# Expert weights loaded as one consecutive 8 KB run per partition, with the features permuted to match

## The chip, the cores and the metric

One program on one core of a Trainium2 chip. The metric is the device time of one execution in microseconds (us), from the first to the last instruction with what lies around them. The core has TensorE (PE; its weight loads are listed apart as PEld), VectorE (DVE), ScalarE (ACT), GpSimd (POOL) and SyncE (SP, which here issues nearly all DMAs), a 128-partition on-chip memory (SBUF), an accumulator memory that PE writes (PSUM), and 16 DMA engines.

## The reference, cut to what matters

One encoder layer over 256 tokens of 1024 features: a norm, three mixing branches, a residual; then a norm, a router and a mixture of 16 experts (4 groups of 4, every token goes to 2 experts of one group), a residual and a last norm. All is float32. The change touches the experts alone:

```python
t = h.reshape(b * s, d)                                   # 256 tokens x 1024
...
for g in range(g_n):                                      # 4 groups
    a = jnp.einsum('td,edf->tef', t, w_gate[g])           # 4 experts x (1024 x 512)
    u = jnp.einsum('td,edf->tef', t, w_up[g])             # 4 experts x (1024 x 512)
    hid = jax.nn.silu(a) * u * combine[:, g, :, None]
    out = out + jnp.einsum('tef,efd->td', hid, w_down[g]) # 4 experts x (512 x 1024)
```

The weights of the 16 experts are 100.7 MB (16 x 3 x 1024 x 512 x 4 bytes) and are read once.

## The kernel before, in words

The program first runs the mixing branches (up to about 300 us). Then it works out the output projection and the router (to about 320 us), and then the experts in 8 pairs `p` (to about 532 us).

**Order of work.** The expert stage is written in program order: every engine runs its instructions in the order of the code. `experts` calls, for each pair, `gate_up` for the even expert, `hidden` of the pair before (PE transposes that turn the activations `gs` so that features lie on partitions, result `hh`), `down` of the pair before, and `gate_up` for the odd expert, with `scatter` and `place` (adding the results back to the tokens' sums) in its middle. After every second pair `gather` makes the four experts' inputs: PE multiplies the normed tokens by a 0/1 matrix `X` and so collects at most 64 tokens for each expert into `xg`, with features on partitions. The normed tokens are kept in two parts, `x1_hi` (written by ACT in `normed_hi`) and `x1_lo` (the rest, written by DVE in `normed_lo`), in tiles C2 and E1; the raw ones are `x1` (tile C1). At the first `gather` all `x1_hi` products run first, then `normed_lo` runs on DVE, then the `x1_lo` products.

**Weights.** A stock of 20 SBUF buffers of 1 MB (8 KB on each partition; tags r0.., B0.., E0.., G.., h0.. and so on) holds weights. `plan` is the list of loads in order of use, one per buffer; `fetch(tag)` issues the next load of the plan into a buffer that has been used up, on SP's queue, and `take` hands out the oldest loaded buffer. A gate/up buffer holds 256 rows of gate and the same 256 rows of up as two DMAs of 512 KB: row r of a 128-row block goes to partition r, so that each run of consecutive bytes in one partition is one row, 2 KB. A down buffer holds 256 rows of 4 KB. `gate_up` takes four buffers in turn and gives each back after its four products (two 128-row blocks, each for gate and up). Gate goes to PSUM partitions 0 to 63 and up to 64 to 127. A float32 product is two PE instructions in the trace, so a buffer is 8 of them. ACT then writes silu of the gate into the tile `gs`, DVE multiplies it by the up part (the last two lines of `gate_up`).

**Before the experts.** SP loads the router's weights (`wr`, 20 columns) around 198 us, DVE scales them by the gain of the norm. The gains lie in `gt` (partition p, column k: feature 128k + p), loaded at the start; `gather` applies the same gain when it moves `xg` out of PSUM.

**The end.** The last pair ends with `down_1` and `scatter_1` over column halves, then `finish` norms the rows and stores them.

Of the kernel before, what the change touches and what calls it, by code (L numbers as in the profile page):

```python
# [9 lines left out]
F32 = mybir.dt.float32  # L10
# [4 lines left out]
AF = mybir.ActivationFunctionType  # L15
ALU = mybir.AluOpType
# [14 lines left out]
def hybrid_encoder_kernel(  # L31
# [112 lines left out]
        plan.pop(0)(raw)  # L144
        ready.append((tag, raw))

    def rows_in(src, parts=1):
        def go(raw):
            dst = raw.rearrange("p (k n) -> p k n", n=src.shape[1])
            k = dst.shape[1] // parts  # L150
            for i in range(parts):
                feeder[0].dma_start(
                    dst[:, i * k : i * k + k], src[i * k * P : (i + 1) * k * P].rearrange("(k p) n -> p k n", p=P)
                )

        return go

# [566 lines left out]
    raw_tags.append("B1")  # L724
    wr = wp.tile([P, KT, 32], F32, tag="gs", name="wr")
    V.memset(wr, 0.0)
    tc.keep_in_program_order(nc.sync.dma_start(wr[:, :, 16:20], w_rg[0].rearrange("(k p) n -> p k n", p=P)))
    tc.keep_in_program_order(nc.sync.dma_start(wr[:, :, 0:16], w_re[0].rearrange("(k p) n -> p k n", p=P)))
    for k in range(KT):
# [34 lines left out]
    def expert_units():  # L764
        us = []

        def gate_and_up(e, r):
            def go(raw):
                for h, w in ((0, w_gate), (1024, w_up)):
                    rows_in(w[e, r : r + 256])(raw[:, h : h + 1024])  # L770

            return go

        def gu(e):
            us.extend(gate_and_up(e, r) for r in range(0, D, 256))

        def dn(*es):
            for r in (0, 256):
                us.extend(rows_in(w_down[e, r : r + 256]) for e in es)

        def dn_cols(e):
            for c in (0, 512):
                us.append(rows_in(w_down[e, :, c : c + 512], 2 if c and e == NE - 1 else 1))

        for p in range(NP):
            gu(2 * p)
            if p:
                dn(2 * p - 2, 2 * p - 1)
            gu(2 * p + 1)
        dn_cols(NE - 2)  # L790
        dn_cols(NE - 1)
        return us
# [181 lines left out]
    x1_hi = slot("C2", [P, 2, D], F32R)  # L974
    x1_lo = slot("E1", [P, 2, D], F32R)

    def normed_hi(a, n):
        ns = slice(n * 512, n * 512 + 512)
        A.activation(x1_hi[:, a, ns], x1[:, a, ns], AF.Copy, scale=r2[:, a : a + 1])

    def normed_lo(a, n):
        ns = slice(n * 512, n * 512 + 512)
        V.scalar_tensor_tensor(
            x1_lo[:, a, ns], x1[:, a, ns], r2[:, a : a + 1], x1_hi[:, a, ns].bitcast(F32), op0=ALU.mult, op1=ALU.subtract
        )

    for a in range(2):
# [128 lines left out]
    def gather(pd, lead=False):  # L1116
        pts = [bank([P, 2, 256]) for _ in range(4)]

        def part(u, x, first):
            for j in range(2):  # L1120
                ks = slice((2 * u + j) * P, (2 * u + j + 1) * P)
                for a in range(2):
                    PE.matmul(
                        pts[u][:, j],
                        x[:, a, ks],
                        pd[:, a].rearrange("p e s -> p (e s)"),
                        start=first and j + a == 0,
                        stop=not first and j + a == 2,
                    )
# [8 lines left out]
        for u in range(4):  # L1138
            pt = pts[u]
            if not lead:  # L1140
                part(u, x1_hi, True)
            part(u, x1_lo, False)
            if u % 2:
                for j in range(2):
                    k = 2 * u + j
                    A.activation(
                        xg[:, k].rearrange("p e s -> p (e s)"), pt[:, j], AF.Copy, scale=gt[:, 3, k : k + 1]
                    )
            else:
                V.tensor_tensor(  # L1150
                    xg[:, 2 * u : 2 * u + 2].rearrange("p k e s -> p k (e s)"),
                    pt,
                    gt[:, 3, 2 * u : 2 * u + 2].unsqueeze(2).to_broadcast([P, 2, 256]),
                    op=ALU.mult,
                )
        return xg
# [22 lines left out]
    def take(n):  # L1179
        tag, raw = ready.pop(0)  # L1180
        return tag, raw.rearrange("p (k n) -> p k n", n=n)

    def gate_up(xg, i, p, gs, between=None):
        pt = bank([P, DFF])
        for u in range(2):
            for h in range(2):
                tag, w = take(DFF)
                for j in range(2):
                    k = 4 * u + 2 * h + j
                    for c in range(2):  # L1190
                        PE.matmul(  # L1191
                            pt[c * 64 : c * 64 + 64], xg[:, k, p % 2 * 2 + i], w[:, 2 * c + j], start=k == 0, stop=k == KT - 1
                        )
                fetch(tag)
            if between and not u:
                between()
        gs = gs or keep([P, DFF], "gs")
        A.activation(gs[64:128], pt[0:64], AF.Silu)  # L1198
        V.tensor_mul(gs[i * 64 : i * 64 + 64], gs[64:128], pt[64:128])  # L1199
        return gs  # L1200

    def down(hs):
# [223 lines left out]
```

## Time and profile before

| | |
|---|---|
| time, median of 3 runs | 545.36 us (545.16 to 545.42) |
| the profiled execution | 545.44 us, span 543.5 us |
| granted PE clock, mean of the span | 0.994 of full speed |
| PE busy | 528.5 us, 97% of the span |
| DVE, ACT, POOL busy | 264.3, 229.0, 18.5 us |
| DMA | 159.91 MB, 89815 packets, mean 294 GB/s |

The span is the time from the first to the last instruction; 1.9 us lie around it. The profile also tells, for every idle stretch of an engine, what ended it, and for every stretch of time how busy the 16 DMA engines were and how many bytes they moved. PE is called busy while a product is in it, so its busy share says that it was fed and not that it ran at its peak.

### The profile page before, as it was taken

The numbers are of one execution on the slowest core, as the hardware profiler recorded it, in microseconds if no ns is written. First come the engines' busy times: TensorE is split into PE (matmuls) and PEld (weight loads), VectorE is DVE, ScalarE is ACT, GpSimd is POOL, SyncE is SP. The second block draws the span as 40 slices with busy tenths as digits, with TensorE's granted clock in tenths as the row PEclk, the third lists the DMA queues.
The fourth block names the chain that finished last, engine by engine and source line by source line (L and its number), as shares of the span: only waits on it lengthen the run. The fifth ranks groups of instructions, "written<-read, shape, count | busy, mean of one in ns | idle before, by whom it ended". The sixth has DMA issues, their size and how long they took to land. (4 is left out here: it accounts for less than half of the span.)

```text
span 543.5 us, 7482 instructions
## 1 busy us (share of the span) xinstructions
PE 528.5 (97%) x2912; PEld 359.9 (66%) x2912; DVE 264.3 (49%) x461; ACT 229.0 (42%) x378; POOL 18.5 (3%) x21
## 2 busy tenths in 40 slices
PE   8999999999999999999999999999999999999992
PEld 6999899967778888888888863353435343534340
DVE  6598798995657768384566171130112111210122
ACT  6775566698654464544535261121111111111123
POOL 0005000040000000000000000000000000000000
PEclk9999999999999999999999999999999999999997
DMA  8987778045445799739983799999999999999962
GB/s 302 390 316 233 224 147 256 17 156 163 148 154 189 235 334 301 257 103 403 354 318 151 275 344 330 416 406 418 406 414 409 409 413 407 416 406 418 406 242 81
DMA packets 89815, 159.91 MB, mean 294 GB/s; under 512 B 13104, under 2 KB 27824, under 8 KB 89776
## 3 DMA queue, kind: packets, MB, share of 16 engines
q1 hardware_dynamic: 89056, 158.80, 80.1%
q10 hardware_dynamic: 720, 0.58, 0.3%
q8 instruction: 25, 0.41, 0.3%
q14 instruction: 14, 0.11, 0.1%
HBM read 158.32 MB, written 1.05 MB: 293 GB/s over the span
## 5 line engine op out<-in xcount | busy, mean ns | idle before, releaser
L129 DVE TENSOR_TENSOR h<-r,h 128x1024 fp32r<-128x1024 f32 x58 | 71.2, 1239 | 31.6 <-ACT h L128 31.2
L128 ACT CAST h<-r 128x1024 fp32r<-128x1024 f32 x58 | 60.2, 1048 | 23.4 <-PE pj L308 12.5
L306 PE MATMUL pj<-h,A 128*128 128x512 f32 x160 | 63.1, 394 | 0.0
L308 PE MATMUL pj<-h,A 128*128 128x512 f32 x160 | 62.7, 392 | 0.0
L307 PE MATMUL pj<-h,A 128*128 128x512 f32 x160 | 62.6, 391 | 0.0
L1199 DVE TENSOR_TENSOR gs<-gs,b 64x512 f32<-64x512 f32 x16 | 11.1, 691 | 87.1 <-ACT gs L1198 87.1
L288 PE MATMUL pj<-A,h 128*128 128x256 f32 x160 | 45.7, 286 | 0.0
L290 PE MATMUL pj<-A,h 128*128 128x256 f32 x160 | 45.5, 284 | 0.0
L289 PE MATMUL pj<-A,h 128*128 128x256 f32 x160 | 45.3, 283 | 0.0
L308 PEld LDWEIGHTS pj<-h,A 128*128 128x128 f32 x160 | 30.1, 188 | 6.9 <-issue 0.8
L306 PEld LDWEIGHTS pj<-h,A 128*128 128x128 f32 x160 | 30.1, 188 | 6.7 <-issue 0.4
L307 PEld LDWEIGHTS pj<-h,A 128*128 128x128 f32 x160 | 30.1, 188 | 6.3 <-DVE h L129 0.4
L1230 DVE SCALAR_TENSOR_TENSOR os<-b,c,os 128x512 fp32r<-128x512 f32 x16 | 12.0, 751 | 41.9 <-ACT os L1229 41.0
L1198 ACT ACTIVATE gs<-b 64x512 f32<-64x512 f32 x16 | 9.4, 588 | 51.8 <-PE b L1191 51.8
L288 PEld LDWEIGHTS pj<-A,h 128*128 128x128 f32 x160 | 30.7, 192 | 0.1
L290 PEld LDWEIGHTS pj<-A,h 128*128 128x128 f32 x160 | 30.7, 192 | 0.1
L289 PEld LDWEIGHTS pj<-A,h 128*128 128x128 f32 x160 | 30.7, 192 | 0.1
L129 DVE TENSOR_TENSOR h<-G,h 128x1024 fp32r<-128x1024 f32 x18 | 24.1, 1346 | 10.3 <-ACT h L128 9.8
L1229 ACT ACTIVATE os<-b,c 128x512 fp32r<-128x512 f32 x16 | 11.0, 687 | 40.6 <-PE b L1210 39.7
L1191 PE MATMUL b<-h,C 128*64 128x512 f32 x104 | 24.0, 592 | 0.0
L128 ACT CAST h<-G 128x1024 fp32r<-128x1024 f32 x18 | 18.8, 1049 | 10.6 <-PE pj L308 9.3
L1210 PE MATMUL b<-h,hh 128*64 128x512 f32 x64 | 21.3, 592 | 0.0
(327 smaller groups left out, 1029.3 us busy)
## 6 DMA issues: line engine op xcount, KB each, us to landing
r<-in_w_in_dram SPq DMA_DIRECT2D x20, 1024.0 KB, 5.4
h<-in_w_exp_down_dram SPq DMA_DIRECT2D x10, 1024.0 KB, 11.5
h<-in_w_exp_gate_dram SPq DMA_DIRECT2D x13, 512.0 KB, 11.0
h<-in_w_exp_up_dram SPq DMA_DIRECT2D x13, 512.0 KB, 11.1
r<-in_w_exp_down_dram SPq DMA_DIRECT2D x6, 1024.0 KB, 11.6
A<-in_w_exp_down_dram SPq DMA_DIRECT2D x5, 1024.0 KB, 11.4
r<-in_w_exp_gate_dram SPq DMA_DIRECT2D x9, 512.0 KB, 10.2
r<-in_w_exp_up_dram SPq DMA_DIRECT2D x9, 512.0 KB, 10.3
```

What stands on the lines that cost most here:

```text
L128: pin(A.copy(hi, part))
L129: pin(V.tensor_sub(lo, part, hi.bitcast(F32)))
L288: PE.matmul(pt, whi[:, cs], thi[:, k], start=k == 0, stop=False)
L289: PE.matmul(pt, whi[:, cs], tlo[:, k], start=False, stop=False)
L290: PE.matmul(pt, wlo[:, cs], thi[:, k], start=False, stop=k == kn - 1)
L306: PE.matmul(pts[a], thi[:, kk, ts], whi, start=first, stop=False)
L307: PE.matmul(pts[a], thi[:, kk, ts], wlo, start=False, stop=False)
L308: PE.matmul(pts[a], tlo[:, kk, ts], whi, start=False, stop=last)
L1191: PE.matmul(pt[c * 64 : c * 64 + 64], xg[:, k, p % 2 * 2 + i], w[:, 2 * c + j], start=k == 0, stop=k == KT - 1)
L1199: V.tensor_mul(gs[i * 64 : i * 64 + 64], gs[64:128], pt[64:128])
L1210: PE.matmul(pts[n][i * 64 : i * 64 + 64], hh[:, 2 * u + k], ws[i][1][:, k, ns], start=u + k == 0, stop=u + k == 2)
L1230: V.scalar_tensor_tensor(o[:, 1], pt, c, o[:, 0].bitcast(F32), op0=ALU.mult, op1=ALU.subtract)
```

## The change

Each DMA of expert weights now gives every partition consecutive rows: partition p of a gate or up buffer gets rows 4p to 4p+3 of a 512-row half (8 KB in one run), and partition p of a down buffer rows 4p + k, with k 0 and 1 or 2 and 3 (two rows of 4 KB that are consecutive). A gate/up buffer now holds 512 rows of gate alone or of up alone, in one DMA of 1 MB, so `gate_up` takes two buffers at once and gives both back after eight products. The last expert pair's down halves still have 2 KB runs (512 columns of a row).

A product needs the same features in the same partitions on both sides. So the features are permuted: in each 512-feature half, `normed_hi` and `normed_lo` read `x1` with a step of four elements (16 bytes) and write `x1_hi` and `x1_lo` in consecutive order, as [4 remainders, 128 quotients]. In the same way the two last lines of `gate_up` read PSUM with a step of four elements and write `gs` in order. The gains in the new order are a new tile `gx` [128, 8], filled by eight DMAs of 32 partitions x 4 elements of 4 bytes each, on SP's queue right ahead of the router's weights.

```diff
--- before.py
+++ after.py
@@ -144,14 +144,12 @@
         plan.pop(0)(raw)
         ready.append((tag, raw))
 
-    def rows_in(src, parts=1):
+    def runs_in(src, parts=1):
         def go(raw):
-            dst = raw.rearrange("p (k n) -> p k n", n=src.shape[1])
+            dst = raw.rearrange("p (k n) -> p k n", n=src.shape[2])
             k = dst.shape[1] // parts
-            for i in range(parts):
-                feeder[0].dma_start(
-                    dst[:, i * k : i * k + k], src[i * k * P : (i + 1) * k * P].rearrange("(k p) n -> p k n", p=P)
-                )
+            for i in range(0, dst.shape[1], k):
+                feeder[0].dma_start(dst[:, i : i + k], src[:, i : i + k])
 
         return go
 
@@ -724,6 +722,11 @@
     raw_tags.append("B1")
     wr = wp.tile([P, KT, 32], F32, tag="gs", name="wr")
     V.memset(wr, 0.0)
+    gx = cp.tile([P, KT], F32, name="gx")
+    for q in range(4):
+        src = gains.rearrange("(p j) c -> p j c", j=4)
+        for u in range(2):
+            pin(nc.sync.dma_start(gx[q * 32 : q * 32 + 32, 4 * u : 4 * u + 4], src[:, :, 24 + 4 * u + q]))
     tc.keep_in_program_order(nc.sync.dma_start(wr[:, :, 16:20], w_rg[0].rearrange("(k p) n -> p k n", p=P)))
     tc.keep_in_program_order(nc.sync.dma_start(wr[:, :, 0:16], w_re[0].rearrange("(k p) n -> p k n", p=P)))
     for k in range(KT):
@@ -764,23 +767,20 @@
     def expert_units():
         us = []
 
-        def gate_and_up(e, r):
-            def go(raw):
-                for h, w in ((0, w_gate), (1024, w_up)):
-                    rows_in(w[e, r : r + 256])(raw[:, h : h + 1024])
-
-            return go
-
         def gu(e):
-            us.extend(gate_and_up(e, r) for r in range(0, D, 256))
+            for r in (0, 512):
+                us.extend(runs_in(w[e, r : r + 512].rearrange("(p j) n -> p j n", j=4)) for w in (w_gate, w_up))
+
+        def by_four(e):
+            return w_down[e].rearrange("(p k) n -> p k n", k=4)
 
         def dn(*es):
-            for r in (0, 256):
-                us.extend(rows_in(w_down[e, r : r + 256]) for e in es)
+            for k in (0, 2):
+                us.extend(runs_in(by_four(e)[:, k : k + 2]) for e in es)
 
         def dn_cols(e):
             for c in (0, 512):
-                us.append(rows_in(w_down[e, :, c : c + 512], 2 if c and e == NE - 1 else 1))
+                us.append(runs_in(by_four(e)[:, :, c : c + 512], 2 if c and e == NE - 1 else 1))
 
         for p in range(NP):
             gu(2 * p)
@@ -974,14 +974,25 @@
     x1_hi = slot("C2", [P, 2, D], F32R)
     x1_lo = slot("E1", [P, 2, D], F32R)
 
+    def fours(t):
+        return t.rearrange("q (p j) -> q j p", j=4)
+
+    def by_p(t):
+        return t.rearrange("q (j p) -> q j p", j=4)
+
     def normed_hi(a, n):
         ns = slice(n * 512, n * 512 + 512)
-        A.activation(x1_hi[:, a, ns], x1[:, a, ns], AF.Copy, scale=r2[:, a : a + 1])
+        A.activation(by_p(x1_hi[:, a, ns]), fours(x1[:, a, ns]), AF.Copy, scale=r2[:, a : a + 1])
 
     def normed_lo(a, n):
         ns = slice(n * 512, n * 512 + 512)
         V.scalar_tensor_tensor(
-            x1_lo[:, a, ns], x1[:, a, ns], r2[:, a : a + 1], x1_hi[:, a, ns].bitcast(F32), op0=ALU.mult, op1=ALU.subtract
+            by_p(x1_lo[:, a, ns]),
+            fours(x1[:, a, ns]),
+            r2[:, a : a + 1],
+            by_p(x1_hi[:, a, ns].bitcast(F32)),
+            op0=ALU.mult,
+            op1=ALU.subtract,
         )
 
     for a in range(2):
...
@@ -1144,13 +1156,13 @@
                 for j in range(2):
                     k = 2 * u + j
                     A.activation(
-                        xg[:, k].rearrange("p e s -> p (e s)"), pt[:, j], AF.Copy, scale=gt[:, 3, k : k + 1]
+                        xg[:, k].rearrange("p e s -> p (e s)"), pt[:, j], AF.Copy, scale=gx[:, k : k + 1]
                     )
             else:
                 V.tensor_tensor(
                     xg[:, 2 * u : 2 * u + 2].rearrange("p k e s -> p k (e s)"),
                     pt,
-                    gt[:, 3, 2 * u : 2 * u + 2].unsqueeze(2).to_broadcast([P, 2, 256]),
+                    gx[:, 2 * u : 2 * u + 2].unsqueeze(2).to_broadcast([P, 2, 256]),
                     op=ALU.mult,
                 )
         return xg
@@ -1183,20 +1195,19 @@
     def gate_up(xg, i, p, gs, between=None):
         pt = bank([P, DFF])
         for u in range(2):
-            for h in range(2):
-                tag, w = take(DFF)
-                for j in range(2):
-                    k = 4 * u + 2 * h + j
-                    for c in range(2):
-                        PE.matmul(
-                            pt[c * 64 : c * 64 + 64], xg[:, k, p % 2 * 2 + i], w[:, 2 * c + j], start=k == 0, stop=k == KT - 1
-                        )
+            ws = [take(DFF) for _ in range(2)]
+            for k in range(4 * u, 4 * u + 4):
+                for c in range(2):
+                    PE.matmul(
+                        pt[c * 64 : c * 64 + 64], xg[:, k, p % 2 * 2 + i], ws[c][1][:, k % 4], start=k == 0, stop=k == KT - 1
+                    )
+            for tag, _ in ws:
                 fetch(tag)
             if between and not u:
                 between()
         gs = gs or keep([P, DFF], "gs")
-        A.activation(gs[64:128], pt[0:64], AF.Silu)
-        V.tensor_mul(gs[i * 64 : i * 64 + 64], gs[64:128], pt[64:128])
+        A.activation(by_p(gs[64:128]), fours(pt[0:64]), AF.Silu)
+        V.tensor_mul(by_p(gs[i * 64 : i * 64 + 64]), by_p(gs[64:128]), fours(pt[64:128]))
         return gs
 
     def down(hs):
```

On PE, at the first `gate_up` of the expert stage (`B`, `E`, `G`, `C` are the first weight buffers, the right-hand `C` is `xg`, `b` a PSUM bank), there stands before:

```order
L1191 MATMUL b_3115<-B_341_2671,C_411_3092 64x512 x4
L1191 MATMUL b_3115<-E_342_2674,C_411_3092 64x512 x4
L1191 MATMUL b_3115<-G_343_2677,C_411_3092 64x512 x4
L1191 MATMUL b_3115<-C_344_2680,C_411_3092 64x512 x4
L1191 MATMUL b_3147<-A_345_2683,C_411_3092 64x512 x4
```

and now:

```order
L1201 MATMUL b_3108<-B_341_2680,C_411_3085 64x512
L1201 MATMUL b_3108<-E_342_2682,C_411_3085 64x512
L1201 MATMUL b_3108<-B_341_2680,C_411_3085 64x512
L1201 MATMUL b_3108<-E_342_2682,C_411_3085 64x512
L1201 MATMUL b_3108<-B_341_2680,C_411_3085 64x512
L1201 MATMUL b_3108<-E_342_2682,C_411_3085 64x512
L1201 MATMUL b_3108<-B_341_2680,C_411_3085 64x512
L1201 MATMUL b_3108<-E_342_2682,C_411_3085 64x512
L1201 MATMUL b_3108<-G_343_2684,C_411_3085 64x512
```

The number of products is the same; two buffers now alternate, so the second one is needed at the second product instead of the fifth, and the first one is held until the eighth.

On SP's queue, at the router's weights (about 198 us; `gx` is the new tile), before:

```order
L121 DMA G_295_2346<-in_w_na_o_dram 128x4x512
L727 DMA wr<-in_w_router_group_dram 128x8x4
L728 DMA wr<-in_w_router_expert_dram 128x8x16
L732 DMA rb<-in_b_router_group_dram 128x4
L733 DMA rb<-in_b_router_expert_dram 128x16
```

and now:

```order
L121 DMA G_295_2346<-in_w_na_o_dram 128x4x512
L729 DMA gx<-in_gains_dram 32x4x1 x8
L730 DMA wr<-in_w_router_group_dram 128x8x4
L731 DMA wr<-in_w_router_expert_dram 128x8x16
L735 DMA rb<-in_b_router_group_dram 128x4
L736 DMA rb<-in_b_router_expert_dram 128x16
```

Eight small DMAs stand ahead of the router's weights and of every load behind them.

On DVE, where the router's weights are scaled (about 207 us; the rows on `h` split weights into two parts for PE, `C` is the retention output, `tri` a constant), before:

```order
L129 TENSOR_TENSOR h_278_2182<-C_277_2180,h_278_2182 128x1024
L604 TENSOR_TENSOR E_196_1630<-pj_2127,E_196_1630 128x512
L730 TENSOR_SCALAR wr<-wr,gt 128x20 x8
L739 CAST tri<-t_300_2402 128x128
L129 TENSOR_TENSOR h_279_2185<-C_277_2180,h_279_2185 128x1024
L604 TENSOR_TENSOR E_196_1630<-pj_2128,E_196_1630 128x512
L693 SCALAR_TENSOR_TENSOR C_261_2065<-at_2155,gt,C_260_2064 128x256
L129 TENSOR_TENSOR h_283_2242<-r_282_2240,h_283_2242 128x1024
```

and now:

```order
L129 TENSOR_TENSOR h_278_2182<-C_277_2180,h_278_2182 128x1024
L602 TENSOR_TENSOR E_196_1630<-pj_2127,E_196_1630 128x512
L129 TENSOR_TENSOR h_279_2185<-C_277_2180,h_279_2185 128x1024
L602 TENSOR_TENSOR E_196_1630<-pj_2128,E_196_1630 128x512
L691 SCALAR_TENSOR_TENSOR C_261_2065<-at_2155,gt,C_260_2064 128x256
L129 TENSOR_TENSOR h_283_2242<-r_282_2240,h_283_2242 128x1024
L691 SCALAR_TENSOR_TENSOR C_261_2065<-at_2155,gt,C_260_2064 128x256
L733 TENSOR_SCALAR wr<-wr,gt 128x20 x5
L691 SCALAR_TENSOR_TENSOR C_261_2065<-at_2155,gt,C_260_2064 128x256
L733 TENSOR_SCALAR wr<-wr,gt 128x20 x3
```

The scaling of `wr` has moved behind five other instructions.

## Rows read from the trace of the kernel before

**Rows 1.** The page: PE's busy time, and GB/s in 40 equal slices.

```profile
PE 528.5 (97%) x2912; PEld 359.9 (66%) x2912; DVE 264.3 (49%) x461; ACT 229.0 (42%) x378; POOL 18.5 (3%) x21
...
GB/s 302 390 316 233 224 147 256 17 156 163 148 154 189 235 334 301 257 103 403 354 318 151 275 344 330 416 406 418 406 414 409 409 413 407 416 406 418 406 242 81
```

**Rows 2.** Waits of PE's weight loads, 325 to 543 us: total, times, longest.

```profile
PEld b L1191 <- issue: 60.9, 216, 0.3
...
PEld b L1210 <- DMA T<-in_w_exp_gate_dram: 0.6, 2, 0.3
```

**Rows 3.** Stretches: length, busy time of engines, PE clock, DMA share, GB/s.

```profile
400.00:405.00 5.00, 5.00 (x26) 1.72 (x24) 0.31 (x1) 0.00 (x0) 0.00 (x0) 1.00 1.03 422
...
425.00:430.00 5.00, 5.00 (x26) 1.64 (x24) 0.69 (x1) 0.59 (x1) 0.00 (x0) 1.00 1.05 404
```

**Rows 4.** Timeline of SP's queue near the end: start, length.

```profile
494.11 4.77 SPq L152 DMA_DIRECT2D h<-in_w_exp_up_dram  x1
```

**Rows 5.** The buffer h loaded then: its DMAs' time to landing.

```profile
DMA to landing us min/median/max: 14.7/14.9/15.1
```

**Rows 6.** Timeline of PE, last pair.

```profile
510.45 1.94 PE L1191 MATMUL b<-G,C 128*64 128x512 f32 x8
...
512.21 1.89 PE L1191 MATMUL b<-h,C 128*64 128x512 f32 x8
```

**Rows 7.** Timeline of PE, start of the experts.

```profile
320.27 2.36 PE L1123 MATMUL b<-X,C 128*128 128x256 f32 x16 [0.83 <-DVE X L1108]
322.47 2.08 PE L1123 MATMUL b<-X,E 128*128 128x256 f32 x16
324.48 1.94 PE L1191 MATMUL b<-B,C 128*64 128x512 f32 x8
```

**Rows 8.** Timeline of ACT, start of the experts.

```profile
314.57 2.56 ACT L979 ACTIVATE C<-C,r 128x512 fp32r<-128x512 f32 x4
```

**Rows 9.** Timeline of DVE, start of the experts.

```profile
319.70 0.76 DVE L1108 TENSOR_TENSOR X<-posm,iota 128x256 fp32r<-128x256 f32 x2
320.38 2.73 DVE L983 SCALAR_TENSOR_TENSOR E<-C,r,C 128x512 fp32r<-128x512 f32 x4
```

**Rows 10.** Timeline of all engines, end of the last pair.

```profile
521.12 0.59 ACT L1198 ACTIVATE gs<-b 64x512 f32<-64x512 f32 x1 [3.12 <-PE b L1191]
...
521.74 0.69 DVE L1199 TENSOR_TENSOR gs<-gs,b 64x512 f32<-64x512 f32 x1 [3.55 <-ACT gs L1198]
...
522.72 0.46 PE L1239 MATMUL b<-ident,gs 64*128 64x64 f32 x4
```

**Rows 11.** Groups by line and shape: busy us, mean ns of one, idle before.

```profile
L129 DVE TENSOR_TENSOR h<-r,h 128x1024 fp32r<-128x1024 f32 x58 | 71.2, 1239 | 31.6 <-ACT h L128 31.2
L128 ACT CAST h<-r 128x1024 fp32r<-128x1024 f32 x58 | 60.2, 1048 | 23.4 <-PE pj L308 12.5 <-PE pj L290 9.2 <-DMA r<-in_w_in_dram 1.1
...
L268 DVE TENSOR_TENSOR h<-r,h 128x512 fp32r<-128x512 f32 x8 | 5.2, 687 | 1.1 <-ACT h L267 1.1
...
L267 ACT CAST h<-r 128x512 fp32r<-128x512 f32 x8 | 4.6, 610 | 1.1 <-DMA r<-in_w_in_dram 1.1
```

**Rows 12.** Two reductions of 16 elements, by line: ns min/median/max.

```profile
L1027 DVE TENSOR_REDUCE pad<-sel x2: 173/176/180, 316.1 to 317.3; 128x4 f32<-128x16 f32 x2
...
L1071 DVE TENSOR_REDUCE cmax<-b x1: 167/167/167, 319.6 to 319.6; 128x1 f32<-128x16 f32 x1
```

**Rows 13.** Timeline of SP's queue behind the router's weights.

```profile
205.58 0.43 SPq L735 DMA_DIRECT2D iota<-in_const_small_dram  x1
...
208.91 0.37 SPq L121 DMA_DIRECT2D B<-in_w_in_dram  x1
```

**Rows 14.** Timeline of ACT, the split of that buffer B.

```profile
232.19 1.04 ACT L128 CAST h<-B 128x1024 fp32r<-128x1024 f32 x1
```

**Rows 15.** DMA issues of the page: KB each, median us to landing.

```profile
r<-in_w_in_dram SPq DMA_DIRECT2D x20, 1024.0 KB, 5.4
```

More of the change, by code (lines that the diff above doesn't have):

```diff
@@ L1120, in part @@
             for j in range(2):
-                ks = slice((2 * u + j) * P, (2 * u + j + 1) * P)
+                k = 2 * u + j
+                ks = slice(k * P, (k + 1) * P)
                 for a in range(2):
```

## The prediction

> **What bounds the kernel now.** I read the page first: PE is busy 97% of the span, and from the 26th of the 40 slices (340 us) to the 38th (516 us) the DMA engines move 406 to 418 GB/s without a break [rows 1]. Both look full, so the question is who waits for whom. The waits of PE's weight loads in the expert stage decide it: the largest entry is 216 gaps of at most 0.3 us with the releaser "issue", PE's own pace, and the largest entry that names a DMA is 0.6 us in all, in two gaps no longer than those [rows 2]. So PE bounds the expert stage, at a granted clock of 1.00 [rows 3], and the DMA engines only have to keep ahead of it. They do so narrowly, since the stock of loaded buffers shrinks towards the end. One of the last loads shows it: the up half of buffer `h` is issued at 494.11 and lands 14.7 to 15.1 us later [rows 4, 5], thus by 509.2; PE begins on this buffer at 512.21 [rows 6]. That is 3.0 us of slack after nearly 200 us of streaming.
>
> **Longer runs, by themselves.** With two sizes of run in the trace their effect can be read. A stretch in which 2 KB rows move makes 404 GB/s at a DMA share of 1.05, and one in which mostly the 4 KB rows of the down weights move makes 422 at 1.03 [rows 3]. What separates them is a fixed cost per run, and another doubling can give back only about half as much again. For 8 KB I estimate 422 to 430 GB/s, against the 406 to 418 of the mix now, or 2 to 4% above its middle. Over the 176 us of full DMA (13 slices of 13.59 us) that puts the loads 4 to 7 us further ahead. It saves PE nothing, since PE does not wait for them. The most that ending all its DMA waits could give is the 0.6 us of [rows 2]. I count 0.
>
> **The coarser hand-over.** Every gate/up product runs as before, in the same number; only the buffers alternate. A step now needs two buffers at its start, where the second came into use one buffer later: 512.21 − 510.45 = 1.76 us [rows 6]. Of the 3.0 us of slack 1.2 are left. The first buffer of each two is also given back up to 1.76 us later. Where loads wait for buffers (the start of the stage) this delays the stream once, so with unchanged bandwidth the slack would be 1.2 − 1.76, about −0.5 us. The estimate of bandwidth covers this many times: 0.
>
> **The eight loads of `gx`.** A small load ahead of it shows SP's price, 0.43 us for `iota` [rows 13]; eight are 3.4 us. The trace has no load of 4-byte pieces, so as the upper bound each may also wait for a 1 MB load ahead of it to land, 5.4 us [rows 15], 8.8 us in all. Behind them stand the router's weights and then the weights in `B`, which SP issues at 208.91 after a wait for the buffer. ACT starts to split `B` at 232.19 [rows 14], 23.3 us later; with 5.4 us to land, 17.9 us are spare, and either bound is covered. DVE now scales `wr` behind five more instructions, so a late `wr` finds it later in line. If DVE did wait there, PE would still have split weights to work on: `hl_pair` has five buffers, and the largest part of ACT's waits ahead of a split, 12.5 of 23.4 us, is for PE to free one [rows 11]. I take 0, and 1 us as the other end.
>
> **The permuted reads.** Four kinds of instruction now read with a step of 16 bytes: `normed_hi` on ACT and `normed_lo` on DVE from SBUF, and the silu on ACT and the product on DVE from PSUM. No long instruction here reads so. From below the cost is nothing: the element count stays, and the writes are in order. From above I take twice the time per element. The price of 512 more elements is on the rows that come in two lengths: DVE 1239 − 687 = 552 ns, ACT 1048 − 610 = 438 ns [rows 11]. What each would do:
>
> - `normed_hi`: four stores begin at 314.57 and take 2.56 us [rows 8]; 4 x 0.44 more ends them at 318.9, before PE's first product with them at 320.27 [rows 7]. Nothing.
> - `normed_lo`: four in 2.73 us from 320.38, so until 323.11 [rows 9]. PE reaches the `x1_lo` products at 322.47 and the second half of them, which need the last two stores, 2.08 / 2 us later, at 323.5 [rows 7]. With 4 x 0.55 the last store ends at 325.3: PE stands still for 1.8 us, and the whole expert stage starts that much later.
> - Silu and product: in the loop PE works for over 3 us on other products before it needs them, two steps of 1.76 [rows 6]; there 1.0 us more is hidden. At the very end it is not: silu from 521.12, the product until 522.43, PE's transposes of the result at 522.72 [rows 10], with `finish` behind them. Of 0.44 + 0.55, about 0.9 us show.
>
> So the bounds are 0 and 1.8 + 0.9 = 2.7 us. There is one short row with this step: a reduction (L1027) of 16 elements, whose inner loop steps over four floats, takes 176 ns; one of 16 consecutive elements (L1071) takes 167 [rows 12]. At twice the time per element, 1.08 ns by the difference above, 17 ns more would be due; 9 are seen, and four results are written instead of one. This is nearer to no cost than to double, but weak, and it says nothing on PSUM. I take 0.
>
> [...]
>
> **The sum.** 0 + 0 + 0 + 0 on the profiled execution's 545.44 us, 0.08 above the median of 545.36: I predict 545.4 us.
>
> **The rivals.**
>
> 1. [...] Both memories dear: 545.4 + 2.7 = 548.1. SBUF alone: 545.4 + 1.8 = 547.2. PSUM alone: 546.3. [...]
> 2. *The DMA engines fall behind* (slower, where I say no change). By the hand-over above it takes a bandwidth less than 0.3% above today's (0.5 of 176 us). If 8 KB runs were 2% slower, 3.5 + 0.5 = 4.0 us of waiting would appear in the last pairs: 549.4. For it: the slack is small and no run here is 8 KB. Against it: 422 over 404.
> 3. *The loads don't get faster*, for instance since an 8 KB run is moved in pieces. Then −0.5 us of slack, at most 545.9. This is inside "no change".
> 4. *Faster.* It needs a wait that the rows don't show, as PE's waits for DMAs are 0.6 us.
>
> **How the numbers follow.** About 0.2% (1.1 us) tells two times of this kernel apart. Chances: no visible cost, rival 3 included, 0.48; SBUF dear, with or without PSUM, 0.30 (547.2 to 548.1); PSUM alone 0.10 (546.3, of which 0.02 pass 1.1 us); the DMA engines behind 0.07; faster 0.05. So faster 0.05, same 0.48 + 0.08 = 0.56, slower 0.30 + 0.02 + 0.07 = 0.39. The range goes from 544.9 to 548.5: it holds the first three cases and leaves out 0.12. The likeliest case alone is 544.9 to 546.0.
>
> **What the changed profile would show.** GB/s of 420 or more where it was 406 to 418, until PE's buffers are all full, and then pauses; the last weights landing earlier than before against PE's last products. The same pace of the products. The durations of the silu (0.59 us), of the product on DVE (0.69), of `normed_lo` and `normed_hi`, unchanged or not, settle rival 1; PE's gap between the `x1_hi` and the `x1_lo` products and before the last transposes shows what it costs. Waits of PE for `w_exp` loads in the last pairs would be rival 2. The forecast is wrong if either is on PE's path by over a microsecond, or if a stretch before 320 us grows: then `gx` was not hidden.

## The result, and the profile after

The changed kernel takes 549.31 us (median of 5 runs, 547.84 to 549.48) against 545.42 us for the kernel before (5 runs, 545.16 to 545.65): 1.0063 times as long, interval 1.0048 to 1.0078. It is slower, by 3.9 us, and outside the range of the prediction. The profiled execution took 548.22 us with a span of 546.2, 2.7 more than before. The rows show where these 2.7 us lie.

The lead of the experts comes first: timelines of ACT, DVE and PE of the changed kernel (start, length, engine, line, what was done, and in brackets the idle time before it).

```profile
316.05 4.54 ACT L985 ACTIVATE C<-C,r 128x512 fp32r<-128x512 f32 x4
```
```profile
321.86 4.26 DVE L989 SCALAR_TENSOR_TENSOR E<-C,r,C 128x512 fp32r<-128x512 f32 x4
```
```profile
321.75 2.36 PE L1135 MATMUL b<-X,C 128*128 128x256 f32 x16 [0.83 <-DVE X L1119]
323.94 1.59 PE L1135 MATMUL b<-X,E 128*128 128x256 f32 x9
326.17 1.09 PE L1135 MATMUL b<-X,E 128*128 128x256 f32 x7 [0.64 <-DVE E L989]
327.20 0.64 PE L1201 MATMUL b<-B,C 128*64 128x512 f32 x1
```

Four `normed_hi` take 4.54 us instead of 2.56 [rows 8], four `normed_lo` 4.26 instead of 2.73 [rows 9], and the `x1_lo` products, 16 in one row before [rows 7], are torn into 9 and 7 with a wait for `normed_lo` between them. From the first `normed_hi` to the first gate/up product it is 327.20 − 316.05 = 11.15 us, and before 324.48 − 314.57 = 9.91 [rows 7, 8]: the lead costs 1.24 us. But `normed_hi` itself begins 1.48 us later, and that loss is older than any line that the change touches.

It is found by walking backwards through the stretches. Ahead of 40 us neither the code nor the order of the loads differs, and yet the loads are slower there. Stretches of the kernel before, and then of the changed one (length, busy time of PE, PEld, DVE, ACT, POOL, PE clock, DMA share, GB/s):

```profile
20.00:35.00 15.00, 14.91 (x123) 14.66 (x123) 10.02 (x16) 9.36 (x15) 0.72 (x1) 1.00 1.08 388
```
```profile
20.00:35.00 15.00, 13.00 (x107) 12.74 (x106) 8.58 (x13) 7.96 (x11) 0.72 (x1) 1.00 1.10 348
340.00:500.00 160.00, 160.00 (x824) 67.07 (x822) 25.84 (x49) 26.70 (x49) 0.00 (x0) 1.00 1.01 420
```

388 GB/s became 348 at a DMA share that is no lower, and PE is busy for 1.91 us less. The waits of the weight loads from 0 to 45 us name the place: one gap of 2.2 us behind DVE's `t` (0.3 before).

```profile
PEld at L237 <- DVE t L232: 2.2, 1, 2.2
```

On DVE, splits of loaded weights `h<-r` run ahead of `t`. Before, and then in the changed kernel (there with the ACT row that they wait for):

```profile
29.96 0.47 DVE L234 TENSOR_SCALAR t<-ident,col 128x128 f32<-128x128 f32 x2
```
```profile
28.11 2.00 ACT L128 CAST h<-r 128x1024 fp32r<-128x1024 f32 x2 [1.10 <-DMA r<-in_w_in_dram]
...
29.19 2.36 DVE L129 TENSOR_TENSOR h<-r,h 128x1024 fp32r<-128x1024 f32 x2 [0.75 <-ACT h L128]
31.47 0.48 DVE L232 TENSOR_SCALAR t<-ident,col 128x128 f32<-128x128 f32 x2
```

ACT waits for a load of `r`, DVE for ACT, and `t` starts 1.51 us later than before.

The rest is as it was. The page of the changed kernel, PE and GB/s in 40 slices, answers to [rows 1]:

```profile
PE 528.7 (97%) x2912; PEld 360.9 (66%) x2912; DVE 265.8 (49%) x461; ACT 231.0 (42%) x378; POOL 18.5 (3%) x21
...
GB/s 296 358 345 220 228 151 245 33 155 155 155 154 177 230 334 152 388 124 398 395 286 149 276 340 272 422 418 421 419 420 418 419 422 419 420 419 420 402 176 81
```

Full streaming is 418 to 422 GB/s, and its last slices read 402 and 176 where they were 406 and 242: the loads end earlier. Of the waits of the weight loads from 325 us on, none with a DMA as its releaser stands among the largest (0.2 us is the longest); the largest group is PE's own pace, as in [rows 2]. Silu and product on PSUM took 0.588 and 0.691 us each before; now, per group:

```profile
L1210 DVE TENSOR_TENSOR gs<-gs,b 64x512 f32<-64x512 f32 x16 | 11.1, 691 | 87.3 <-ACT gs L1209 87.3
...
L1209 ACT ACTIVATE gs<-b 64x512 f32<-64x512 f32 x16 | 9.4, 590 | 52.2 <-PE b L1201 52.2
```

The silu at the very end answers to [rows 10]:

```profile
523.83 0.59 ACT L1209 ACTIVATE gs<-b 64x512 f32<-64x512 f32 x1 [3.12 <-PE b L1201]
```

It starts 523.83 − 327.20 = 196.63 us after the first gate/up product, and before 521.12 − 324.48 = 196.64: the expert stage itself takes as long as it did. So the whole loss of the profiled run lies ahead of it, 1.48 + 1.24 = 2.72 us.

SP spends 9.06 us on the eight loads of `gx`, and issues `B` at 213.56 instead of 208.91 [rows 13]:

```profile
200.10 9.06 SPq L729 DMA_DIRECT2D gx<-in_gains_dram  x8
...
213.56 0.41 SPq L121 DMA_DIRECT2D B<-in_w_in_dram  x1
```

### The profile page after: what moved, and what is told of

Its sections match the earlier page's. It is cut to its first block, busy times and chain, and to the rows that moved or that the text cites. A ratio compares the mean times of both kernels' runs of the same rounds, so it can differ in the third digit from the quotient of the medians.

```text
span 546.2 us, 7415 instructions
## 1 busy us (share of the span) xinstructions
PE 528.7 (97%) x2912; PEld 360.9 (66%) x2912; DVE 265.8 (49%) x461; ACT 231.0 (42%) x378; POOL 18.5 (3%) x21
## 5 line engine op out<-in xcount | busy, mean ns | idle before, releaser
L1201 PE MATMUL b<-h,C 128*64 128x512 f32 x104 | 39.6, 594 | 0.0
L1201 PE MATMUL b<-B,C 128*64 128x512 f32 x64 | 29.0, 596 | 0.0
L1201 PE MATMUL b<-G,C 128*64 128x512 f32 x64 | 29.0, 596 | 0.0
```

What stands on the lines that cost most here:

```text
L1201: PE.matmul(pt[c * 64 : c * 64 + 64], xg[:, k, p % 2 * 2 + i], ws[c][1][:, k % 4], start=k == 0, stop=k == KT - 1)
```

## The experiments

### What belongs to the change: both kernels again, and x1 in order

The first suspicion for the slow start was the chip, since the two profiles need not come from the same one. So both kernels were run unchanged side by side, with one more in which the lead's reads with a step are taken back.

> The kernel before, unchanged, profiled on the same chip as the three kernels that follow, since the two profiles at hand differ in a place where the code is the same: in 0 to 40 us the changed kernel's PE was busy for 1.9 us less, with loads that moved more slowly, and everything to the experts was 1.47 us later. If that belongs to the chip of the day, this profile shows the slower start too (attention's end and the x1 stage about 1.5 us later than in the first profile, span about 545); if it belongs to the change, this profile repeats the first one, span 543.5 within 0.4.

> The changed kernel, unchanged, beside it. Lead theory: normed_hi and normed_lo, read with a step of 16 bytes, take 4.5 and 4.3 us for four, and PE's first gate/up product comes 1.25 us later after the start of the lead than before; that is all that the change costs, so if the early start is the chip's, before and after differ by 1.2 to 1.4 us (ratio 1.0024). Rival: about 1.5 us of the loss lies ahead of 40 us and comes with the change as well, so the ratio repeats 1.006 and this profile again has some 1.5 us more than the profile of before on the same chip at the start of normed_hi.

```
# e3, in normed_hi and normed_lo
-        A.activation(by_p(x1_hi[:, a, ns]), fours(x1[:, a, ns]), AF.Copy, ...)
+        A.activation(x1_hi[:, a, ns], x1[:, a, ns], AF.Copy, ...)
-            by_p(x1_lo[:, a, ns]), fours(x1[:, a, ns]), r2[...], by_p(x1_hi[...]),
+            x1_lo[:, a, ns], x1[:, a, ns], r2[...], x1_hi[...],
```

> The changed kernel with one part undone: normed_hi and normed_lo read x1 in order and write in order (the features of x1_hi and x1_lo are then not permuted, so the expert sums mix the wrong features; all counts, sizes and loads stay). Lead theory: four normed_hi take 2.6 us and four normed_lo 2.7 us again, the wait of 0.6 us ahead of PE's x1_lo products goes, and the kernel is 1.2 to 1.4 us faster than the changed one. If the lead is all of the loss, it equals the kernel before (within 0.5 us). Rival (loss ahead of 40 us comes with the change, by its loads or its program): it keeps 1.5 us or more of the loss, 547 us or more.

Measured: before 544.94 us in its profiled run and 545.45 as the median beside these kernels; the changed kernel 548.38, ratio 1.0053 (1.0038 to 1.0068); x1 in order 548.70, ratio 1.0057 (1.0043 to 1.0071). First `normed_hi` and first gate/up product of e1, e2 and e3:

```profile
314.32 2.56 ACT L979 ACTIVATE C<-C,r 128x512 fp32r<-128x512 f32 x4
...
324.23 1.94 PE L1191 MATMUL b<-B,C 128*64 128x512 f32 x8
```
```profile
316.06 4.53 ACT L985 ACTIVATE C<-C,r 128x512 fp32r<-128x512 f32 x4
...
327.22 0.64 PE L1201 MATMUL b<-B,C 128*64 128x512 f32 x1
```
```profile
316.69 2.56 ACT L985 ACTIVATE C<-C,r 128x512 fp32r<-128x512 f32 x4
...
326.60 0.64 PE L1201 MATMUL b<-B,C 128*64 128x512 f32 x1
```

The chip is not the cause: e1 begins `normed_hi` at 314.32, e2 at 316.06 on the same chip. In e3 the lead is back to 326.60 − 316.69 = 9.91 us, exactly as before, so the reads with a step are all of the lead's 1.24. The time is another matter: the 1.2 to 1.4 us that were expected do not show. In the profiles half of them are lost again, since e3 begins the lead 0.63 us later than e2 (316.69 and 316.06); the rest is less than the spread of these few runs (e3 547.22 to 549.19, e2 547.97 to 548.53). What the lead costs by the clock is settled further down (e6 and e9). The larger part of the loss lies ahead of 40 us and comes with the change by some way that its instructions don't show.

### The permutation moved to PE

```
# e4: normed_hi and normed_lo as in e3, and in gather
-                ks = slice(k * P, (k + 1) * P)
+                ks = slice(k // 4 * 512 + k % 4, k // 4 * 512 + 512, 4)
```

> All of the change, computing the same result, but with the features permuted at another place: normed_hi and normed_lo read and write in order, and PE's gather takes every fourth column of x1_hi and x1_lo as its stationary operand instead of 128 consecutive ones. Lead theory: if the weight load with a step of 16 bytes costs nothing or is hidden beside the products (64 loads, each beside a product of 256 columns), this is 1.2 to 1.4 us faster than the changed kernel, and the same as the one with x1 in order. If the weight load pays as DVE and ACT did (half as long again, or three quarters), PE's lead products at two chunks, and those of three more gathers, become longer: 64 products in all, a cost of 0.05 us each would be 3 us.

Measured: 562.72 us, ratio 1.0315 (1.0300 to 1.0329). Weight loads and products of the `x1_hi` half, grouped (busy us, mean ns of one), first of e4 and then of the changed kernel, e2:

```profile
L1135 PEld LDWEIGHTS b<-X,C 128*128 128x128 f32 x64 | 16.2, 328 | 3.4 <-issue 2.4 <-ACT e L1076 0.9
...
L1135 PE MATMUL b<-X,C 128*128 128x256 f32 x64 | 17.6, 404 | 0.8 <-DVE X L1119 0.8
```
```profile
L1135 PEld LDWEIGHTS b<-X,C 128*128 128x128 f32 x64 | 8.6, 190 | 3.5 <-issue 2.4 <-ACT e L1076 0.9
...
L1135 PE MATMUL b<-X,C 128*128 128x256 f32 x64 | 10.4, 289 | 0.8 <-DVE X L1119 0.8
```

A weight load of 128 columns with a step of 16 bytes takes 328 ns instead of 190, longer than the 289 ns that a product of 256 columns took beside it, and each product takes 115 ns more (404 instead of 289). There are 128 such products (64 with `x1_hi`, 64 with `x1_lo`; the expectation counted only one half): 14.7 us as an estimate, and 562.72 − 548.38 = 14.34 us were lost. Of the three engines PE is the worst to read this step here, 14.34 us against the lead's 1.24 on ACT and DVE, since it repeats the read for each of the four gathers.

### Where the buffers lie

What the instructions don't show, the allocation does. `gx` is a tile of 32 bytes per partition in the pool that lies ahead of the pool of large buffers, so every large buffer moves by 32 bytes. In the built program the first of them, `E0`, starts at these bytes of a partition, and the others follow at multiples of 8192 (a trace shows no addresses; the shifts follow from the sizes of the tiles):

```
before 19968 = 39 x 512         changed kernel 20000 (+32)
e5  before, +32   20000         e6  changed, gx of 512 bytes   20480 (+512)
e7  changed, gx of 64 bytes     20032 (+64)
e11 before, +256  20224         e12 before, +128  20096
```

```
# e5 (8 floats), e11 (64 floats), e12 (32 floats): the kernel before
+    gap = cp.tile([P, 8], F32, name="gap")
     sp = ctx.enter_context(tc.tile_pool(name="sp", bufs=1))
# e6 (128 floats), e7 (16 floats): the changed kernel
-    gx = cp.tile([P, KT], F32, name="gx")
+    gx = cp.tile([P, 128], F32, name="gx")
```

> The kernel before with one unused tile of 32 bytes per partition allocated ahead of the pool of the large buffers, and nothing else: no instruction is added or moved. In the program the large buffers of the kernel before start at multiples of 512 bytes of a partition (19968, 28160, ...); the tile `gx` of the change, 32 bytes, moves all of them to 20000, 28192, ..., 32 beyond a multiple of 64. Placement theory: this shift makes the loads of the first 40 us slower (344 to 350 GB/s in the 5 us windows from 20 to 35 us, where the kernel before has 379 to 397), so this kernel is 1.2 to 2.0 us slower than the kernel before (546.6 to 547.5), with products in order. Rival (the slow start comes with something else of the change, such as fewer and longer runs in the program): 545.4, and 379 to 397 GB/s.

> All of the change, computing the same result, with `gx` allocated as 512 bytes per partition (only its first 32 are used), so that the large buffers start at multiples of 512 again. Placement theory: the start is as in the kernel before (379 to 397 GB/s from 20 to 35 us, normed_hi at 314.3 to 314.6), and only the lead's 1.25 us is left: 546.4 to 546.9, and the expert stage streams at more than the 418 to 422 of the changed kernel. Rival (not the placement): 548 to 549 as the changed kernel.

> The same with 64 bytes: the large buffers start at 64 beyond a multiple of 512. If what counts is a multiple of 64, it repeats the run with 512 bytes (546.4 to 546.9); if it takes a larger unit, it is as slow as the changed kernel (548 to 549), or between.

> The kernel before with an unused tile of 256 bytes, so that the large buffers start at 256 beyond a multiple of 512. With 32 bytes the same edit cost 8.5 us; with 64 the changed kernel was as slow as with 32. If 256 is unit enough, this takes 545.4; if the unit is 512, about 553.9; if the loss grows with the share of runs that cross a line, between.

> The kernel before with an unused tile of 128 bytes, so that the large buffers start at 128 beyond a multiple of 256. With 32 bytes the same edit cost 8.5 us, with 256 nothing; the changed kernel was as slow with 64 as with 32. If 128 is unit enough, this takes 545.4 and has 379 to 398 GB/s from 20 to 35 us; if the unit is 256, it is as slow as with 32 bytes, about 553.9, with 344 to 350 GB/s there.

Measured, with the ratio to the kernel before:

```
e5  before, +32    553.86 us   1.0146 (1.0132 to 1.0159)
e12 before, +128   551.44 us   1.0108 (1.0091 to 1.0125)
e11 before, +256   545.41 us   0.9999 (0.9990 to 1.0008)
e7  changed, +64   549.32 us   1.0060 (1.0043 to 1.0076)
e6  changed, +512  546.80 us   1.0028 (1.0019 to 1.0037)
```

The same two stretches of each, in the order e5, e12, e11, e7, e6:

```profile
20.00:35.00 15.00, 12.78 (x97) 12.52 (x96) 8.84 (x13) 7.97 (x11) 0.71 (x1) 0.93 1.10 347
340.00:500.00 160.00, 160.00 (x824) 67.08 (x822) 25.85 (x49) 26.69 (x49) 0.00 (x0) 1.00 1.04 394
```
```profile
20.00:35.00 15.00, 13.05 (x108) 12.79 (x107) 8.98 (x13) 7.78 (x11) 0.72 (x1) 1.00 1.10 348
340.00:500.00 160.00, 160.00 (x824) 67.02 (x822) 25.84 (x49) 26.69 (x49) 0.00 (x0) 1.00 1.04 397
```
```profile
20.00:35.00 15.00, 14.82 (x122) 14.56 (x121) 9.73 (x16) 9.37 (x15) 0.71 (x1) 1.00 1.08 388
340.00:500.00 160.00, 160.00 (x824) 67.14 (x822) 25.77 (x49) 26.28 (x49) 0.00 (x0) 1.00 1.04 412
```
```profile
20.00:35.00 15.00, 13.06 (x101) 12.81 (x100) 9.03 (x13) 7.89 (x11) 0.71 (x1) 0.94 1.10 347
340.00:500.00 160.00, 160.00 (x824) 67.08 (x822) 25.31 (x49) 26.52 (x50) 0.00 (x0) 1.00 1.01 421
```
```profile
20.00:35.00 15.00, 14.81 (x122) 14.56 (x121) 9.89 (x17) 9.43 (x15) 0.72 (x1) 1.00 1.08 387
340.00:500.00 160.00, 160.00 (x822) 66.85 (x818) 25.83 (x49) 26.70 (x49) 0.00 (x0) 1.00 1.01 427
```

The rows fall into two groups. With buffers at multiples of 256 bytes the start moves 387 or 388 GB/s, and the expert stage 412 with the kernel before (e11) and 427 with the 8 KB runs. Beyond a multiple of 256 by 32, 64 or 128 bytes they are 347 or 348, and 394 to 397 or 420 to 421. An unused tile, without one instruction, makes the kernel before 8.5 us slower. The theory of placement holds, and 64 bytes are not unit enough, 128 neither, 256 are. Two sizes were missed: e5 was expected at 546.6 to 547.5, and e12, if 128 bytes fell short, at the 553.9 of e5.

What e5's expectation left out is the expert stage. In e5 and e12 PE runs into the DMA engines there, between 506 and 515 us (waits of the weight loads: total, times, longest; e5, then e12):

```profile
PEld b L1211 <- DMA r<-in_w_exp_down_dram: 5.1, 3, 2.6
```
```profile
PEld b L1211 <- DMA r<-in_w_exp_down_dram: 4.0, 3, 2.3
```

In e5 the first gate/up product comes at 327.12, 2.64 us late, and these waits add 5.1: 7.7 of the 8.4 us by which its span is longer. In e12 it comes at 326.20, 1.72 late, and the waits add 4.0: 5.7 of 5.8.

In e7 no such wait is among the largest, though its buffers lie as badly: its 8 KB runs still move 421 GB/s. So the change has its worth there: moved by 32 bytes, it takes 548.4 to 549.3 us where the kernel before takes 553.9 (e5).

What a packet, one run of bytes, loses is read where the same mix of packets moves. First the start, 20 to 30 us, before and changed; then 2 KB rows, 425 to 430 us, before and e5; then the 8 KB runs, 340 to 500 us, e6 and the changed kernel:

```profile
DMA packets 3912, 3.82 MB, mean 382 GB/s; under 512 B 200, under 2 KB 3911, under 8 KB 3911
```
```profile
DMA packets 3563, 3.47 MB, mean 347 GB/s; under 512 B 195, under 2 KB 3562, under 8 KB 3562
```
```profile
DMA packets 1043, 2.02 MB, mean 404 GB/s; under 512 B 63, under 2 KB 63, under 8 KB 1042
```
```profile
DMA packets 1004, 1.93 MB, mean 387 GB/s; under 512 B 60, under 2 KB 60, under 8 KB 1004
```
```profile
DMA packets 9361, 68.26 MB, mean 427 GB/s; under 512 B 1035, under 2 KB 1035, under 8 KB 1035
```
```profile
DMA packets 9219, 67.17 MB, mean 420 GB/s; under 512 B 1026, under 2 KB 1026, under 8 KB 1026
```

With 16 engines at work all the time that is 40.9 and 44.9 ns for a packet, 76.7 and 79.7, 273.5 and 277.7: an estimate of 3 to 4 ns for each, whatever its length.

So these runs show a unit of 256 bytes and not 64 or 128 (e7, e12 and e11: 347, 348 and 388 GB/s at the start), and a price for each run and not for each byte. What was moved is the written side, SBUF; how the loss comes about, no run shows.

### The permutation at the writes, and the sum closed

```
# e8: e6, and normed_hi and normed_lo run over x1 in order and write x1_hi and x1_lo with a step of 512 bytes
-        A.activation(by_p(x1_hi[...]), fours(x1[...]), AF.Copy, ...)      # q (j p) -> q j p;  q (p j) -> q j p
+        A.activation(by_j(x1_hi[...]), as_read(x1[...]), AF.Copy, ...)    # q (j p) -> q p j;  q (p j) -> q p j
# e9: e6 and e3 together
```

> The run with 512 bytes, and the features permuted at the writes: normed_hi reads x1 in order and writes x1_hi with a step of 512 bytes, and normed_lo reads x1 in order, reads x1_hi with a step of 512 bytes and writes x1_lo so. The result is the same. If only reads with a step cost and writes do not, four normed_hi take 2.6 us instead of 4.5; normed_lo still reads one of its operands with a step, and takes about 4.3. If what costs is a step in either direction, normed_hi stays at 4.5. If the cost grows with the step (16 bytes before, 512 now), normed_lo takes more than 4.3 and PE's first gate/up product comes later than in the run with 512 bytes; time 546.4 to 548.

> The changed kernel with `gx` allocated as 512 bytes and with x1 read and written in order (the features of x1_hi and x1_lo are then not permuted, so the expert sums mix the wrong features; all counts, sizes and loads stay). If placement (about 1.5 us and more) and the lead's reads with a step (1.25 us) are all that the change costs, this takes 545.2 to 545.7, the time of the kernel before, and the eight loads of `gx`, the hand-over of two buffers and the reads of PSUM with a step cost nothing. Rival (one of those three costs too): 546 or more, and the loss shows between the first gate/up product and the end, or between 200 and 240 us.

Measured: e8 546.69 us, ratio 1.0024 (1.0015 to 1.0033); e9 545.47 us, ratio 1.0002 (0.9993 to 1.0010). Four `normed_hi` and four `normed_lo` of e8, then the first gate/up product of e6 and that of e9:

```profile
314.26 4.03 ACT L991 ACTIVATE C<-C,r 128x512 fp32r<-128x512 f32 x4
...
320.06 4.27 DVE L995 SCALAR_TENSOR_TENSOR E<-C,r,C 128x512 fp32r<-128x512 f32 x4
```
```profile
325.68 0.64 PE L1201 MATMUL b<-B,C 128*64 128x512 f32 x1
```
```profile
324.36 0.64 PE L1201 MATMUL b<-B,C 128*64 128x512 f32 x1
```

Writes with a step are not free on ACT either: 4.03 us against 4.54 with reads and 2.56 in order. DVE takes 4.27 with one operand and the result stepping by 512 bytes, as long as with one operand stepping by 16; neither guess of the expectation (free writes, or a cost that grows with the step) held in full.

e9 closes the sum. With the placement mended and x1 in order, nothing is left: 545.47 against 545.42. So the eight loads of `gx`, the hand-over by two buffers and the stepped reads of PSUM cost nothing together, within −0.4 and 0.5 us, and neither do the longer runs gain anything. Two that cancel are unlikely: silu and product are as long as before, and a gain would need waits for DMAs, of which there were 0.6 us. The lead's reads cost 546.80 − 545.47 = 1.33 us by the clock, 325.68 − 324.36 = 1.32 in these rows. The placement costs the rest, 549.31 − 546.80 = 2.5 us by the first comparison, 548.38 − 546.80 = 1.6 by the second. The profiles show 1.48 and 1.74 us of it, by which `normed_hi` begins later in the changed kernel and in e2.

### The lead mended

```
# e10: e6, normed_hi writes with a step as in e8, and
+    def scaled(a, n):                      # on ACT, for three of the four parts
+        A.activation(by_j(xs[a][:, ns]), as_read(x1[:, a, ns]), AF.Copy, scale=r2[:, a : a + 1])
...
+        if a or n:
+            V.tensor_sub(x1_lo[:, a, ns], xs[a][:, ns], x1_hi[:, a, ns].bitcast(F32))
+            return
```

> All of the change, the same result, `gx` allocated as 512 bytes, and the lead rearranged: ACT permutes at its writes (four normed_hi in about 4.0 us) and, while it has nothing else to do, also writes the scaled x1 for three of the four parts to the buffers `os`, so that DVE only subtracts there, with all operands in order (about 0.7 us each instead of 1.07). Lead theory: four normed_lo take 1.07 + 3 x 0.7 = 3.2 us instead of 4.3, the last is ready 3.2 us after `X`, when PE gets to its second half, and the wait of 0.65 us goes: 545.3 to 545.8. If ACT's later table load and evictions or DVE's subtraction are late instead, some of the 1.25 us stays: 546 to 547. Not faster than the kernel before, since there is no other wait to take away.

Measured: 546.11 us, ratio 1.0015 (1.0006 to 1.0023). DVE's four parts and PE's first gate/up product:

```profile
320.22 1.15 DVE L1004 SCALAR_TENSOR_TENSOR E<-C,r,C 128x512 fp32r<-128x512 f32 x1
321.29 1.89 DVE L1002 TENSOR_TENSOR E<-os,C 128x512 fp32r<-128x512 f32 x3
```
```profile
324.32 0.64 PE L1218 MATMUL b<-B,C 128*64 128x512 f32 x1
```

The time lies between the two cases of the expectation. The four parts take 3.0 us and the wait is gone; the first gate/up product comes at 324.32, as in e9. By the clock it saves 0.7 us of the 1.3. In the two profiles the engines run alike from there to the last store, which ACT issues at 537.15 and at 537.18 in e9, so where the other 0.6 us lie stays open. No version beats the kernel before: it had almost no wait for a DMA to lose (0.6 us, [rows 2]).

## Why the prediction was wrong, step by step

**What bounds the kernel: right.** PE does, and faster loads gave nothing: e9, with 427 GB/s where e11 has 412, takes 545.47 us against its 545.41.

**Longer runs, 0 us, 422 to 430 GB/s: right** for buffers at multiples of 256 bytes, with 427 in e6. In the changed kernel as it stands 420 were left, for the reason below.

**The coarser hand-over, 0: right** (e9, and no wait of PE for a DMA above 0.2 us).

**The loads of `gx`, 0: wrong in what was counted.** The step costed what SP does with them, "either bound is covered". SP's 9.06 us passed the upper bound of 8.8 a little and were hidden, as e9 shows. What was missing is the tile itself: its 32 bytes put every large buffer off the 256-byte grid. This is the larger part of the loss, 1.6 to 2.5 us, and it has no term in the sum and no rival: the step looked at what the change issues and not at what it allocates. The test given for this step, a stretch before 320 us that grows, did fire, but by another cause: the stretch that grew lies 165 us ahead of the loads.

**The permuted reads, "I take 0": wrong for SBUF, right for PSUM.** `normed_lo` pays 0.38 us more each ((4.26 − 2.73) / 4), of a bound of 0.55; PE's delay is 1.24 us, of a bound of 1.8. `normed_hi` pays 0.495 us, above the bound of 0.44, and is hidden as predicted. The step that failed is the reading of the short reduction [rows 12]. 9 of 17 ns is a little over half, and not "nearer to no cost than to double". Carried over to 512 elements, 9 / 16 ns each are an estimate of 0.29 us for one `normed_lo` and 1.15 for four, with the last store at 324.3, 0.8 us after PE wants it; measured were 0.38 / 512 = 0.75 ns for an element. The row was weak, but it spoke for a cost, and the sum took 0. Silu and product pay 2 and 0 ns (590 and 691 against 588 and 691). So the step of 16 bytes cost where it was read from SBUF, on ACT (4.54 us for four against 2.56), on DVE (4.26 against 2.73) and in PE's weight load (328 ns against 190, e4), and not where ACT and DVE read it from PSUM.

**The rivals.** The first, SBUF alone dear, was right in place and sign: 547.2 forecast, 546.8 measured in e6. The second, DMA engines that fall behind, did not happen here, but e5 and e12 show the mechanism as costed: a bandwidth lower by 4% became waits of 4 to 5 us towards the end (for e5, with the 3.0 us of slack of the kernel before, the rival's own sum gives 0.044 x 176 − 3.0 = 4.7; 5.1 were measured). In the changed kernel, with buffers as badly placed, 420 GB/s were enough.

**The range** ended at 548.5 because the two mishaps add: 545.4 + 1.3 + 1.6 to 2.5 = 548.3 to 549.2. Only one of them was in the list. This sum closes by the way in which the placement was priced, as what is left over e6; the check that does not is in the rows, 543.5 + 1.48 + 1.24 = 546.2, the span of the changed kernel. Its median is 1.1 us above that profiled run, and this stays open.

## What to carry to other kernels

A diff's allocations are part of the change: list what a new tile moves, and keep buffers that DMAs write at multiples of 256 bytes (here 256 bytes cost nothing, 128 cost 5.8 us and 32 cost 8.5 of the kernel before, e11, e12 and e5). A small tile in a pool ahead of them cost more here, 1.6 to 2.5 us, than the loads that fill it, which cost nothing visible (e9). When a stretch grows in which no line has changed, compare its GB/s before looking for a cause further on. A transposing read should be put where it reads PSUM, which was free here (0 and 2 ns), or where the engine waits anyway; in SBUF a step of 16 bytes made these instructions half as long again on DVE (4.26 us instead of 2.73) and three quarters longer on ACT (4.54 instead of 2.56) and PE's weight load (328 ns instead of 190).

## What the runs showed of the hardware that was not expected

- An unused tile of 32 bytes cost 8.5 us of 545, and one of 256 bytes nothing (e5, e11). The loss is an estimated 3 to 4 ns for each run, so it is 9% of the GB/s for the short runs of the start (382 to 347) and 1.6% for 8 KB (427 to 420).
- A weight load of 128 columns with a step of 16 bytes took 328 ns instead of 190 (e4); ACT's stepped write took 4.03 us for four, its stepped read 4.54, in order 2.56 (e8, e6, e9).
- In e5 and e7 the granted clock of 20 to 35 us is 0.93 and 0.94, where PE stood still for 2.4 and 2.1 us behind the late loads; in e12 and the changed kernel, with 2.2 us, it stayed at 1.00. In e7 `normed_hi` then begins at 317.28 instead of 316.06. The five runs of the changed kernel sort by the clock too, 547.84 and 548.22 us at a mean of 0.995 and 0.993, 549.31 to 549.48 at 0.989 to 0.992; that it is this drop was not tested.
